# Shifting the start of each weight piece inside its buffers, in a gated-convolution layer on one core

## The chip, the cores and the metric

The kernel runs on one core of a Trainium2 chip. A core has a matrix engine (TensorE, in the profile PE for matmuls and PEld for the loading of the stationary operand), VectorE (DVE), ScalarE (ACT), GpSimd (POOL) and the queue processor SyncE (SP), which here issues all transfers (DMA) between the main memory and the on-chip memory. Matmuls write to eight accumulation banks. The metric is the device time of one execution in microseconds; the time before is the median of three runs.

## The reference

One layer of a decoder trunk, for 256 positions and a model width of 2048. In short, with `D = 2048`, `E = 4096`, one layer and float32 throughout:

```python
h = rmsnorm(x, norm_g)
mod = silu(c) @ ada_w + ada_b            # (1, 3*D): shift, scale, gate
h = h * (1 + scale) + shift
b_gate, c_gate, v, g = split(h @ w_in, 4)         # w_in (D, 4*E)
u = causal_depthwise_conv(c_gate * v, conv_w)     # three taps
y = (b_gate * u * silu(g)) @ w_out                # w_out (E, D)
out = rmsnorm(x + gate * y, final_g)
```

The large inputs are `w_in` (2048 x 16384), `w_out` (4096 x 2048) and `ada_w` (2048 x 6144), all float32. All the weights are read once.

## The kernel before

**Precision.** TensorE multiplies in a float32 form with a shortened mantissa (F32R). So each float32 operand is split into a high part, its rounded value, and a low part, the rest; the product is hi·hi + hi·lo + lo·hi, that is three matmuls' worth of columns. `split` does it for a piece of weights of up to 2048 floats per partition: ScalarE casts `raw` into `hi` (L191), VectorE subtracts `hi` from `raw` into `lo` (L192). `raw`, `hi` and `lo` have three buffers each. The normalized and modulated input lies transposed in `hT`, per block k of 128 channels first the 256 columns of the high part, then those of the low part.

**Stages.** At the start x is loaded, normalized (without shift and scale) and transposed by TensorE into `xs`. Then come three stages.

1. *mm_s*, the first 16 of 32 channel tiles of each quarter of `w_in`, in parts of four tiles (function `part`). A part runs over some range of k, so that it can begin before all of `hT` is known. Weights `hi` and `lo` are the stationary operand, `hT` streams in 256 columns: L286 (hi with the high half of hT), L291 (hi with the low half), L292 (lo with the high half). Partial sums are added up in `acc` (L298, L300). Meanwhile the adaLN product for shift and scale is computed on VectorE, from pieces `at` of `ada_w` (loaded at L231; multiplied by silu(c) and added into `gv` at L236 and L238), summed over partitions by transposing (L247) and accumulating on ScalarE (L249). A group of one or two blocks k is then scaled, shifted and split into `hT` (L258, L261, L262). The function `plan` writes the order of adaLN pieces and matmul parts out beforehand, by costs and due times of its own.
2. *mm_b*, the other 16 tiles, two tiles and one quarter at a time over all of k: L382 streams 512 columns of `hT` (both halves) against hi, L385 streams 256 against lo. The gating and convolution follow per pair of tiles. Between them stand the adaLN pieces for the gate (`at_g`, issued at L350, used at L357 and L359).
3. *mm_o*, the product with `w_out`. Here the roles change: `y` is the stationary operand and the weights stream in 512 columns: L427 (high part of y with hi), L428 (high part of y with lo), L429 (low part of y with hi). Then the gated residual and the last norm.

**Buffers.** On-chip memory is handed out pool after pool, from the left and from the right end. From the left: constants (`const`), then `adap` with two `gv` and four `at` buffers of 4 KB a partition, then `wpool` with three buffers each of `raw`, `lo` and `hi`, 8 KB a partition. From the right end down: `hpool` (32 KB: `hT`, later `big`) and `slots` (4 KB each: `xs`, `acc`, `y`, `z`, gates). In the first group of adaLN pieces (k0 = 0) the buffers of `lo` and `hi` serve as `at0`, since no weights need them yet. Nearly all of the memory is in use.

**Order.** Within each engine the order is fixed when the program is built, by a list scheduler that simulates the timeline; the scheduler also sees how many buffers a pool has. SP issues transfers in order, so that a transfer whose buffer isn't free yet holds up those behind it. The lines that matter here are L191 and L192 in `split`, L231 to L238 in `ada_piece`, L273 (load of `raw_s`), L350 (load of `at_g`), and the matmul lines above.

Of the kernel before, what the change touches and what calls it, by code (L numbers as in the profile page):

```python
# [8 lines left out]
F32 = mybir.dt.float32  # L9
F32R = mybir.dt.float32r  # L10
# [3 lines left out]
P = 128  # L14
# [20 lines left out]

SLOT = 2048
ASLOT = 1024
NSLOT = KT // CT + 4 * NCH


# [48 lines left out]
def short_conv_layer(ctx: ExitStack, tc: tile.TileContext, x, c, norm_g, ada_w, ada_b, w_in, conv_w, w_out, final_g, out):  # L89
    nc = tc.nc  # L90
    PSUM = bass.MemoryType.PSUM

    const = ctx.enter_context(tc.tile_pool(name="const", bufs=1))
    adap = ctx.enter_context(tc.tile_pool(name="adap", bufs=2))
    wpool = ctx.enter_context(tc.tile_pool(name="wpool", bufs=2))
    psum = ctx.enter_context(tc.tile_pool(name="psum", bufs=6, space=PSUM))
    hpool = ctx.enter_context(tc.tile_pool(name="hpool", bufs=1, side="right"))
    slots = ctx.enter_context(tc.tile_pool(name="slots", bufs=NSLOT, side="right"))

# [84 lines left out]
    shift = const.tile([P, KT], F32, tag="shift", name="shift")  # L184
    scale = const.tile([P, KT], F32, tag="scale", name="scale")

    def split(raw, n):

        hi = wpool.tile([P, SLOT], F32R, tag="hi", name="hi", bufs=3)
        lo = wpool.tile([P, SLOT], F32R, tag="lo", name="lo", bufs=3)  # L190
        nc.scalar.copy(hi[:, :n], raw[:, :n])  # L191
        nc.vector.tensor_tensor(out=lo[:, :n], in0=raw[:, :n], in1=hi[:, :n].bitcast(F32), op=ALU.subtract)  # L192
        return hi, lo
# [22 lines left out]
    def ada_piece(k0, nk, piece):  # L216
        w = nk * P
        kk = ASLOT // (2 * w)
        if piece == 0:
            sums[k0] = adap.tile([P, 2, 2 * P], F32, tag="gv", name="gv")  # L220
        gv = sums[k0]

        turns = [gv[:, :, i * w : (i + 1) * w] for i in range(2 if k0 == 0 and nk == 1 else 1)]
        j = piece * kk
        if k0 == 0:
            at = wpool.tile([P, SLOT], F32, tag=("lo", "hi")[piece % 2], name="at0", bufs=3)[:, :ASLOT]
        else:
            at = adap.tile([P, ASLOT], F32, tag="at", name="at", bufs=4)
        at4 = at.rearrange("p (k s f) -> p k s f", k=kk, s=2)
        for s in range(2):  # L230
            nc.sync.dma_start(at4[:, :, s, :], adas[:, j : j + kk, s, k0 * P : k0 * P + w])  # L231
        for i in range(kk):
            c_k = silu_c[:, j + i : j + i + 1]
            g2 = turns[(j + i) % len(turns)]
            if j + i < len(turns):
                nc.vector.tensor_scalar_mul(g2, at4[:, i], c_k)  # L236
            else:
                nc.vector.scalar_tensor_tensor(out=g2, in0=at4[:, i], scalar=c_k, in1=g2, op0=ALU.mult, op1=ALU.add)  # L238
        if j + kk < KT:
            return  # L240
        if len(turns) == 2:
            nc.vector.tensor_tensor(out=turns[0], in0=turns[0], in1=turns[1], op=ALU.add)

        tp = psum.tile([P, 4, P], F32, tag="sm", name="tp_g", bufs=2)
        gs = const.tile([P, 4], F32, tag="gs", name="gs", bufs=2)
        for o in range(2 * nk):
            nc.tensor.transpose(tp[:, o, :], gv[:, o // nk, (o % nk) * P : (o % nk + 1) * P], ident)  # L247
        for o in range(2 * nk):
            nc.scalar.activation(gjunk, tp[:, o, :], AF.Copy, accum_out=gs[:, o : o + 1])  # L249
        ks = slice(k0, k0 + nk)  # L250
        nc.vector.tensor_tensor(out=scale[:, ks], in0=gs[:, nk : 2 * nk], in1=b_scale[:, ks], op=ALU.add)
        nc.vector.tensor_tensor(out=shift[:, ks], in0=gs[:, 0:nk], in1=b_shift[:, ks], op=ALU.add)
        nc.vector.scalar_tensor_tensor(
            out=scale[:, ks], in0=scale[:, ks], scalar=1.0, in1=gT[:, ks], op0=ALU.add, op1=ALU.mult
        )
        for k in range(k0, k0 + nk):
            hf = xs[k // CT][:, k % CT, :]
            nc.vector.tensor_scalar(  # L258
                out=hf, in0=hf, scalar1=scale[:, k : k + 1], scalar2=shift[:, k : k + 1], op0=ALU.mult, op1=ALU.add
            )  # L260
            nc.scalar.copy(hh_[:, k], hf)  # L261
            nc.vector.tensor_tensor(out=hl_[:, k], in0=hf, in1=hh_[:, k].bitcast(F32), op=ALU.subtract)  # L262

    def part(ch, q, k0, k1):
# [4 lines left out]
        for s0 in range(k0, k1, step):  # L269
            sk = min(step, k1 - s0)  # L270
            n = sk * CT * P
            raw = raw_tile("raw_s")
            nc.sync.dma_start(  # L273
                raw[:, :n].rearrange("p (k f) -> p k f", k=sk),
                w_in[0, s0 * P : (s0 + sk) * P, col : col + CT * P].rearrange("(k p) f -> p k f", p=P),
            )
            hi, lo = split(raw, n)
            for i in range(sk):
                k = s0 + i
                hh, hl = hh_[:, k], hl_[:, k]  # L280
                for m in range(CT):
                    o = slice((i * CT + m) * P, (i * CT + m + 1) * P)
                    dst = banks[m // 2][:, (m % 2) * T : (m % 2 + 1) * T]

                    opens = k == k0 and m % 2 == 0
                    first = nc.tensor.matmul(dst, hi[:, o], hh, start=opens, stop=False, skip_group_check=True)  # L286
                    if opens:
                        opener = first
                    elif k == k0:
                        tc.add_manual_dep(first.ins, opener.ins.name, after, reason="the bank's flags are cleared first")  # L290
                    nc.tensor.matmul(dst, hi[:, o], hl, start=False, stop=False, skip_group_check=True)  # L291
                    nc.tensor.matmul(dst, lo[:, o], hh, start=False, stop=k == k1 - 1, skip_group_check=True)  # L292
# [25 lines left out]
    for kind, *step in plan():  # L318
        if kind == "ada":
            ada_piece(*step)  # L320
        else:
            ch, k1 = step[0], step[3]
            part(*step)
            whole[ch] += k1 == KT
            if k1 == KT and whole[ch] == 4:
                mixed(ch)
# [11 lines left out]
    def gate(dc):  # L338
        return gates[dc // 2][:, dc % 2, :]
# [4 lines left out]
    def gate_piece():  # L344
        if not gate_todo:
            return
        dc, j = gate_todo.pop(0)
        at = adap.tile([P, ASLOT], F32, tag="at", name="at_g", bufs=4)
        at3 = at.rearrange("p (k f) -> p k f", k=2)
        nc.sync.dma_start(at3, adas[:, j : j + 2, 2, dc * 512 : (dc + 1) * 512])  # L350
        if j == 0:
            gacc[0] = adap.tile([P, 512], F32, tag="gv", name="gacc")
        ga = gacc[0]
        for i in range(2):
            s = silu_c[:, j + i : j + i + 1]
            if j + i == 0:
                nc.vector.tensor_scalar_mul(ga, at3[:, i, :], s)  # L357
            else:
                nc.vector.scalar_tensor_tensor(out=ga, in0=at3[:, i, :], scalar=s, in1=ga, op0=ALU.mult, op1=ALU.add)  # L359
        if j + 2 == KT:  # L360
            ps = psum.tile([P, 512], F32, tag="sm", name="ps_gate", bufs=2)
            nc.tensor.matmul(ps, ones, ga, start=True, stop=True)  # L362
            nc.vector.tensor_tensor(out=gate(dc), in0=ps, in1=gate(dc), op=ALU.add)
# [3 lines left out]
    for ct in range(NS, NCT, 2):  # L367
        for q in QUARTERS:
            banks = [psum.tile([P, 2, T], F32, tag="mm", name="mm_b") for _ in range(2)]
            col = q * E + ct * P  # L370
            for kp in range(0, KT, KP):
                raw = raw_tile("raw")
                nc.sync.dma_start(
                    raw.rearrange("p (k f) -> p k f", k=KP),
                    w_in[0, kp * P : (kp + KP) * P, col : col + 2 * P].rearrange("(k p) f -> p k f", p=P),
                )
                hi, lo = split(raw, SLOT)
                for m in range(2):
                    for i in range(KP):
                        k = kp + i  # L380
                        o = slice((i * 2 + m) * P, (i * 2 + m + 1) * P)
                        nc.tensor.matmul(  # L382
                            banks[m].rearrange("p a t -> p (a t)"), hi[:, o], hT[:, k, :], start=k == 0, stop=False, skip_group_check=True
                        )
                        nc.tensor.matmul(banks[m][:, 0, :], lo[:, o], hh_[:, k], start=False, stop=k == KT - 1, skip_group_check=True)  # L385
                n_piece += 1
                if n_piece % 2 == 0:
                    gate_piece()
# [17 lines left out]
    while gate_todo:  # L406
        gate_piece()
# [41 lines left out]
    for dc in range(4):  # L449
# [8 lines left out]
        for ep in range(n_ep):  # L458
# [11 lines left out]
            hi, lo = split(raw, SLOT)  # L470
# [55 lines left out]
```

## Time and profile before

| | |
|---|---|
| median of three runs | 953.21 us (949.77 to 953.99) |
| profiled execution | 952.04 us, span 950.2 us, mean granted clock 0.99 |
| TensorE busy (matmuls) | 918.3 us, 97% of the span |
| weight loads busy | 835.4 us, 88% |
| VectorE, ScalarE busy | 681.4 us (72%), 419.3 us (44%) |
| transfers | 227.51 MB, mean 239 GB/s, 72.9% of the 16 DMA engines |
| mm_s, mm_b, mm_o | from 27 to 407 us, to 763 us, to 941 us |

How to read it: times are microseconds from the start of the span. A row of a group gives line, engine, operation, output and inputs by the program's names, shapes, count, then the busy time, the mean length of one in ns, and the idle time of the engine just before such instructions with what ended it. Matmuls are pipelined: the length of one reaches into the next, so the cost of a matmul in a row of them is the distance from its start to the next one's. The row of slices has one digit for each fortieth of the span, the busy share in tenths. In a row of windows stand the stretch, its length, busy time and count, the granted clock of TensorE, the share of the DMA engines in use and the rate.

### The profile page before, as it was taken

The numbers are of one execution on the slowest core, as the hardware profiler recorded it, in microseconds if no ns is written. First come the engines' busy times: TensorE is split into PE (matmuls) and PEld (weight loads), VectorE is DVE, ScalarE is ACT, GpSimd is POOL, SyncE is SP. The second block draws the span as 40 slices with busy tenths as digits, with TensorE's granted clock in tenths as the row PEclk, the third lists the DMA queues.
The fourth block names the chain that finished last, engine by engine and source line by source line (L and its number), as shares of the span: only waits on it lengthen the run. The fifth ranks groups of instructions, "written<-read, shape, count | busy, mean of one in ns | idle before, by whom it ended". The sixth has DMA issues, their size and how long they took to land.

```text
span 950.2 us, 14332 instructions
## 1 busy us (share of the span) xinstructions
PE 918.3 (97%) x5963; PEld 835.4 (88%) x5963; DVE 681.4 (72%) x789; ACT 419.3 (44%) x470; POOL 0.7 (0%) x6
## 2 busy tenths in 40 slices
PE   2799999999999999999999999999999999999996
PEld 2699999999999999988888888888888878888885
DVE  4799998999999998997465556555555654544882
ACT  6575343443435544444443444444444433343333
POOL 0000000000000000000000000000000000000000
PEclk9799999999999999999999999999999999999998
DMA  9999997999989787886665565566555685555542
GB/s 273 299 360 368 291 335 253 323 347 319 350 278 308 243 271 240 281 288 208 193 201 181 185 199 193 178 193 201 181 178 190 206 313 177 180 199 196 178 133 88
DMA packets 172048, 227.51 MB, mean 239 GB/s; under 512 B 5792, under 2 KB 112464, under 8 KB 171600
## 3 DMA queue, kind: packets, MB, share of 16 engines
q1 hardware_dynamic: 171984, 226.61, 72.9%
q8 instruction: 46, 0.75, 0.3%
q14 instruction: 18, 0.15, 0.0%
HBM read 224.49 MB, written 2.10 MB: 238 GB/s over the span
## 4 chain that ended last, share of the span: by engine, by line
PE 91%; DMA 4%; DVE 2%; issue 1%; SPq 1%; ACT 0%; ACTq 0%; DVEq 0%
PE mm_b L382 25%; PE mm_b L385 13%; PE mm_s L292 11%; PE mm_s L286 11%; PE mm_s L291 11%; PE mm_o L428 6%; PE mm_o L427 6%; PE mm_o L429 6%; DMA at<-in_ada_w_dram 2%; DMA raw_s<-in_sc_w_in_dram 2%; DVE lo L192 1%; DMA x<-in_x_dram 1%; DVE gv L238 1%; SPq L231 0%; PE ps_gate L362 0%
## 5 line engine op out<-in xcount | busy, mean ns | idle before, releaser
L382 PE MATMUL mm_b<-hT,hi 128*128 128x512 f32 x1024 | 355.2, 392 | 0.0
L286 PE MATMUL mm_s<-hT,hi 128*128 128x256 f32 x1024 | 286.9, 284 | 7.5 <-ACT hT L261 4.9
L291 PE MATMUL mm_s<-hT,hi 128*128 128x256 f32 x1024 | 287.7, 283 | 0.0
L385 PE MATMUL mm_b<-hT,lo 128*128 128x256 f32 x1024 | 285.4, 280 | 0.0
L292 PE MATMUL mm_s<-hT,lo 128*128 128x256 f32 x1024 | 283.6, 283 | 1.7 <-DVE lo L192 1.7
L192 DVE TENSOR_TENSOR lo<-raw,hi 128x2048 fp32r<-128x2048 f32 x64 | 146.6, 2291 | 128.4 <-ACT hi L191 128.4
L382 PEld LDWEIGHTS mm_b<-hT,hi 128*128 128x128 f32 x1024 | 192.0, 188 | 42.3 <-issue 0.2
L191 ACT CAST hi<-raw_s 128x2048 fp32r<-128x2048 f32 (+3 forms) x85 | 126.5, 1488 | 177.1 <-PE mm_s L291 128.6
L286 PEld LDWEIGHTS mm_s<-hT,hi 128*128 128x128 f32 x1024 | 194.4, 191 | 8.5 <-ACT hT L261 5.1
L291 PEld LDWEIGHTS mm_s<-hT,hi 128*128 128x128 f32 x1024 | 195.5, 191 | 0.2 <-issue 0.2
L292 PEld LDWEIGHTS mm_s<-hT,lo 128*128 128x128 f32 x1024 | 192.6, 191 | 2.6 <-DVE lo L192 2.4
L385 PEld LDWEIGHTS mm_b<-hT,lo 128*128 128x128 f32 x1024 | 192.3, 188 | 0.5 <-issue 0.2
L191 ACT CAST hi<-raw 128x2048 fp32r<-128x2048 f32 x64 | 122.4, 1912 | 158.0 <-PE mm_b L382 103.1
L192 DVE TENSOR_TENSOR lo<-raw_s,hi 128x2048 fp32r<-128x2048 f32 (+3 forms) x85 | 149.5, 1759 | 19.9 <-ACT hi L191 19.5
L192 DVE TENSOR_TENSOR lo<-raw_o,hi 128x2048 fp32r<-128x2048 f32 x32 | 73.3, 2290 | 67.0 <-ACT hi L191 67.0
L191 ACT CAST hi<-raw_o 128x2048 fp32r<-128x2048 f32 x32 | 61.2, 1913 | 103.8 <-PE mm_o L429 93.6
L428 PE MATMUL mm_o<-lo,y 128*128 128x512 f32 x256 | 101.7, 399 | 0.0
L427 PE MATMUL mm_o<-hi,y 128*128 128x512 f32 x256 | 101.0, 396 | 0.0
L429 PE MATMUL mm_o<-hi,y 128*128 128x512 f32 x256 | 100.1, 392 | 0.0
L238 DVE SCALAR_TENSOR_TENSOR gv<-at,silu_c,gv 128x512 f32<-128x512 f32 (+1 forms) x149 | 92.2, 639 | 3.8 <-DMA at<-in_ada_w_dram 3.0
L427 PEld LDWEIGHTS mm_o<-hi,y 128*128 128x128 f32 x256 | 48.1, 188 | 12.6 <-issue 0.2
L429 PEld LDWEIGHTS mm_o<-hi,y 128*128 128x128 f32 x256 | 48.1, 188 | 11.6
(84 smaller groups left out, 457.8 us busy)
## 6 DMA issues: line engine op xcount, KB each, us to landing
raw<-in_sc_w_in_dram SPq DMA_DIRECT2D x64, 1024.0 KB, 5.6
raw_s<-in_sc_w_in_dram SPq DMA_DIRECT2D x46, 1024.0 KB, 7.3
at<-in_ada_w_dram SPq DMA_DIRECT2D x128, 256.0 KB, 6.7
raw_o<-in_sc_w_out_dram SPq DMA_DIRECT2D x32, 1024.0 KB, 5.1
at_g<-in_ada_w_dram SPq DMA_DIRECT2D x32, 512.0 KB, 6.9
raw_s<-in_sc_w_in_dram SPq DMA_DIRECT2D x19, 512.0 KB, 5.4
raw_s<-in_sc_w_in_dram SPq DMA_DIRECT2D x7, 768.0 KB, 7.7
raw_s<-in_sc_w_in_dram SPq DMA_DIRECT2D x13, 256.0 KB, 4.4
```

Source lines behind the costliest of these rows:

```text
L191: nc.scalar.copy(hi[:, :n], raw[:, :n])
L192: nc.vector.tensor_tensor(out=lo[:, :n], in0=raw[:, :n], in1=hi[:, :n].bitcast(F32), op=ALU.subtract)
L238: nc.vector.scalar_tensor_tensor(out=g2, in0=at4[:, i], scalar=c_k, in1=g2, op0=ALU.mult, op1=ALU.add)
L286: first = nc.tensor.matmul(dst, hi[:, o], hh, start=opens, stop=False, skip_group_check=True)
L291: nc.tensor.matmul(dst, hi[:, o], hl, start=False, stop=False, skip_group_check=True)
L292: nc.tensor.matmul(dst, lo[:, o], hh, start=False, stop=k == k1 - 1, skip_group_check=True)
L382: nc.tensor.matmul(banks[m].rearrange("p a t -> p (a t)"), hi[:, o], hT[:, k, :], start=k == 0, stop=False, skip_group_check=True)
L385: nc.tensor.matmul(banks[m][:, 0, :], lo[:, o], hh_[:, k], start=False, stop=k == KT - 1, skip_group_check=True)
L427: nc.tensor.matmul(po, yh, hi[:, o], start=opens, stop=False, skip_group_check=True)
L428: nc.tensor.matmul(po, yh, lo[:, o], start=False, stop=False, skip_group_check=True)
L429: nc.tensor.matmul(po, yl, hi[:, o], start=False, stop=ct == NCT - 1, skip_group_check=True)
```

## The change

A piece of weights used to begin at the beginning of its `hi` and `lo` buffer. Now these buffers are 64 floats (256 bytes) longer, and a counter in `split` sets where a piece begins: `hi` at 0, 8, 16, ... 56 floats, a new place with each piece; `lo` at the same eight places, a new one with every eighth piece. There are 181 pieces in all, so all 64 pairs of places come up. The matmuls take their slices from the shifted view. To make room, the `at` buffers of adaLN are three where they were four. Two tiles that nothing uses are added: 224 bytes a partition at the right end of the memory, so that `hT` and the slots move down by that much, and 192 bytes after the constants, so that the pools from `adap` on move up.

```diff
+LEFT = 48
+LINE = 64
...
+    lines = ctx.enter_context(tc.tile_pool(name="lines", bufs=1, side="right"))
+    lines.tile([P, 56], F32, tag="end", name="end")
     const = ctx.enter_context(tc.tile_pool(name="const", bufs=1))
+    linel = ctx.enter_context(tc.tile_pool(name="linel", bufs=1))
+    linel.tile([P, LEFT], F32, tag="begin", name="begin")
     adap = ctx.enter_context(tc.tile_pool(name="adap", bufs=2))
...
+    n_split = [0]
+
     def split(raw, n):
 
-        hi = wpool.tile([P, SLOT], F32R, tag="hi", name="hi", bufs=3)
-        lo = wpool.tile([P, SLOT], F32R, tag="lo", name="lo", bufs=3)
+        o, n_split[0] = n_split[0], n_split[0] + 1
+        ho, lo = o % 8 * 8, o // 8 % 8 * 8
+        hi = wpool.tile([P, SLOT + LINE], F32R, tag="hi", name="hi", bufs=3)[:, ho : ho + SLOT]
+        lo = wpool.tile([P, SLOT + LINE], F32R, tag="lo", name="lo", bufs=3)[:, lo : lo + SLOT]
         nc.scalar.copy(hi[:, :n], raw[:, :n])
...
         if k0 == 0:
-            at = wpool.tile([P, SLOT], F32, tag=("lo", "hi")[piece % 2], name="at0", bufs=3)[:, :ASLOT]
+            at = wpool.tile([P, SLOT + LINE], F32, tag=("lo", "hi")[piece % 2], name="at0", bufs=3)[:, :ASLOT]
         else:
-            at = adap.tile([P, ASLOT], F32, tag="at", name="at", bufs=4)
+            at = adap.tile([P, ASLOT], F32, tag="at", name="at", bufs=3)
...
-        at = adap.tile([P, ASLOT], F32, tag="at", name="at_g", bufs=4)
+        at = adap.tile([P, ASLOT], F32, tag="at", name="at_g", bufs=3)
```

## The prediction

> **What bounds the kernel now.** First the page: busy shares, slices, the chain that ended last.
>
> ```profile
> span 950.2 us, 14332 instructions
> PE 918.3 (97%) x5963; PEld 835.4 (88%) x5963; DVE 681.4 (72%) x789; ACT 419.3 (44%) x470; POOL 0.7 (0%) x6
> ...
> PE   2799999999999999999999999999999999999996
> ...
> DVE  4799998999999998997465556555555654544882
> ...
> PE 91%; DMA 4%; DVE 2%; issue 1%; SPq 1%; ACT 0%; ACTq 0%; DVEq 0%
> ```
>
> TensorE is busy from the second slice to the last and holds 91% of the chain, so what is added to every matmul comes out at the end, and what is added elsewhere counts only once a matmul waits for it. VectorE is full for the first 16 slices or so: there, work that comes late may reach TensorE. Next the groups, shapes apart.
>
> ```profile
> L382 PE MATMUL mm_b<-hT,hi 128*128 128x512 f32 x1024 | 355.2, 392 | 0.0
> L291 PE MATMUL mm_s<-hT,hi 128*128 128x256 f32 x1024 | 287.7, 283 | 0.0
> L286 PE MATMUL mm_s<-hT,hi 128*128 128x256 f32 x1024 | 286.9, 284 | 7.5 <-ACT hT L261 4.9 <-ACT hi L191 2.6
> L385 PE MATMUL mm_b<-hT,lo 128*128 128x256 f32 x1024 | 285.4, 280 | 0.0
> L292 PE MATMUL mm_s<-hT,lo 128*128 128x256 f32 x1024 | 283.6, 283 | 1.7 <-DVE lo L192 1.7
> ...
> L428 PE MATMUL mm_o<-lo,y 128*128 128x512 f32 x256 | 101.7, 399 | 0.0
> L427 PE MATMUL mm_o<-hi,y 128*128 128x512 f32 x256 | 101.0, 396 | 0.0
> L429 PE MATMUL mm_o<-hi,y 128*128 128x512 f32 x256 | 100.1, 392 | 0.0
> ```
>
> The idle columns tell that matmuls hardly wait: 7.5 + 1.7 us for all that use hT. The means overlap one another, so the cost of one is the step from start to start. Stages by windows (columns: us, PE busy and count, granted clock, DMA share, GB/s):
>
> ```profile
> 28.60:33.00 4.40, 4.40 (x22) 0.50 0.81 243
> ...
> 420.00:670.00 250.00, 250.00 (x1444) 1.00 0.61 196
> 770.00:925.00 155.00, 155.00 (x666) 1.00 0.57 193
> ```
>
> A window also counts a matmul or two that reach over its edges. Then mm_b takes 250/1442 = 173.4 ns a matmul, 346.7 for a pair of 512 and 256 columns, and mm_o 155/664 = 233.4. For mm_s and for the pure streaming time I read starts in the timeline (start us, length; first and last of each run):
>
> ```profile
> 28.78 0.41 PE L291 MATMUL mm_s<-hT,hi 128*128 128x256 f32 x1
> ...
> 30.06 0.41 PE L292 MATMUL mm_s<-hT,lo 128*128 128x256 f32 x1
> ...
> 101.25 0.28 PE L292 MATMUL mm_s<-hT,lo 128*128 128x256 f32 x1
> ...
> 102.43 0.28 PE L286 MATMUL mm_s<-hT,hi 128*128 128x256 f32 x1
> ...
> 249.83 0.28 PE L292 MATMUL mm_s<-hT,lo 128*128 128x256 f32 x1
> ...
> 250.79 0.28 PE L291 MATMUL mm_s<-hT,hi 128*128 128x256 f32 x1
> ...
> 281.77 0.28 PE L292 MATMUL mm_s<-hT,lo 128*128 128x256 f32 x1
> ...
> 282.84 0.28 PE L292 MATMUL mm_s<-hT,lo 128*128 128x256 f32 x1
> ```
>
> Six steps at the granted clock 0.50 take 1.28 us, 213.3 ns each; at the full clock that is 106.7 ns for 256 columns and 213.3 for 512. At the full clock the three other runs show 1.18/10 = 118, 0.96/8 = 120 and 1.07/9 = 119 ns. So beside its streaming a matmul pays an extra: about 12.2 ns in mm_s, 26.7/2 = 13.3 in mm_b, 233.4 - 213.3 = 20 in mm_o. In all 3072 x 12.2 + 2048 x 13.3 + 768 x 20 = 37.5 + 27.2 + 15.4 = 80 us, which is all that any place of the operands could give back. The three rhythms of mm_s came with one layout, so places are not all that sets them.
>
> **The change part by part.** Sums stand against the profiled execution, 952.04 us with its span of 950.2; the median of the runs is 953.21, 1.2 higher.
>
> *What is not added.* No matmul, cast, subtraction or transfer is added or taken away; buffer counts of raw, hi and lo stay. The two unused tiles have no instruction. The cast (L191) and the subtraction (L192) write to shifted places with the same shapes; I cost that at nothing, for after the first 16 slices VectorE is busy four to six tenths, ScalarE is busy 44% of the span, and the waits for hi and lo above are all that ever reached a matmul.
>
> *Places.* Adding up the tiles by the code, hT and y begin today 32 bytes past a multiple of 64, hi and lo on one. Afterwards hT and y begin on a multiple of 256; a piece's hi and lo begin 0, 32, ... 224 bytes past one, so half the places lie on a multiple of 64 and half between. No row shows the same shape in another layout. The nearest: in mm_o the loaded side (y) lies between and the streamed side (hi, lo) on a multiple, at 20 ns; in mm_s and mm_b it is the other way round, at 12 to 13. Read that way, loading from between costs 20 - 12.2 = 7.8 ns in mm_s and 6.7 in mm_b: 3072 x 7.8 + 2048 x 6.7 = 38 us if all pieces paid it, 19 for the half that begin between. mm_o would gain 768 x 6.7 = 5, its loaded side now being on a multiple. That makes +14. The stages differ in width too, so the reading may be wrong and the price zero; I take half, **+7 us**. Ends: +38, all places as dear as mm_o; below, one step of 7 ns (L428's mean 399 less L429's 392) off each of the 5120 matmuls that stream hT, -36.
>
> *Three adaLN buffers.* Rows for the loop of one buffer:
>
> ```profile
> at<-in_ada_w_dram SPq DMA_DIRECT2D x128, 256.0 KB, 6.7
> ...
> L231 SPq DMA_DIRECT2D at<-in_ada_w_dram x128: 367/460/1427, 4.9 to 234.8; - x128
> ...
> 112.64 0.75 DVE L238 SCALAR_TENSOR_TENSOR gv<-at,silu_c,gv 128x512 f32<-128x512 f32 x1
> ...
> 113.42 0.88 SPq L231 DMA_DIRECT2D at<-in_ada_w_dram  x2
> ...
> 118.57 2.28 DVE L192 TENSOR_TENSOR lo<-raw_s,hi 128x2048 fp32r<-128x2048 f32 x1
> ...
> L238 DVE SCALAR_TENSOR_TENSOR gv<-at,silu_c,gv 128x512 f32<-128x512 f32 (+1 forms) x149 | 92.2, 639 | 3.8 <-DMA at<-in_ada_w_dram 3.0
> ...
> 55.00:250.00 195.00, 177.97 (x230) 1.00 0.97 325
> ```
>
> The issue at 113.42 starts as the vector operation of 112.64 ends (113.39): SP waits for the buffer. 64 pieces go out in 230 us, 3.6 us each, so a buffer's loop is 14.4 us with four buffers. Of it 0.9 is issue, 6.7 landing, two operations of 0.75 use: 9.1. The other 5.3 us the piece lies waiting for VectorE's turn. With three buffers the same pace leaves a loop of 10.8 and a wait of 1.7, which is less than one subtraction (2.28) ahead of it in VectorE's queue: short by 0.6 us a loop, 0.2 a piece, 10 us over the 50 pieces from 55 us on. Queued behind a late piece's operations are subtractions that feed TensorE, and behind its issue on SP are the raw_s loads; DMA is full there too (share 0.97), so a held-up issue isn't all made up for. Against it: VectorE still has 195 - 178 = 17 us idle in that stretch, and VectorE idled only 3.8 us for at with four. So 0 if VectorE's waiting takes all of it, 10 if nothing does; I take **+4 us**, close to what at costs VectorE today. The gate pieces use the same buffers, but their sums are read only in the output stage, which the last window above shows: nothing.
>
> Sum: 952.0 + 7 + 4 = **963 us**, 1.0% above the median of the runs.
>
> **The rivals.** *Places cost nothing.* For it: the three rhythms under one layout. Against it: mm_o's 20 ns. Time: 952 plus 0 to 4 for the buffers, 952 to 956, which I count as no change. The Trainium skill, page SBUF — State Buffer, section Door 1: The DMA port swizzle, says that consecutive accesses pay for each new 16-byte line; all places of the change are multiples of 32 bytes, so by that rule no stream touches more lines than before, and 956 would be the sum where mine is 963. Its page TensorE: Matmul & The Clock Gate, section Back-to-back issue gap, would give 109 ns for 256 columns; the trace has 118 to 120 and doesn't agree, so something that those rules leave out is at work.
>
> *Faster: hT on the boundary.* The matmuls that stream hT lose one 7 ns step wherever the loaded piece begins on a multiple of 64 too, in half the pieces: 2560 x 7 = 18 us, less the 4 of the buffers: 938. For it: today every one of these 5120 streams begins between two multiples, and the 7 ns step exists (L428 against L429). Against it: mm_o streams from a multiple and has the larger extra. It decides as soon as the step saved in some places outweighs what the others add, at an average of 1 ns a matmul (5 us).
>
> *Much slower: the places collide.* All eight are as dear as mm_o: 952 + 38 + 4 = 994; half of that price: 975. *adaLN becomes the bound* in the first 250 us: the 10 us in full and as much again because the raw_s loads behind it on SP land late: 952 + 7 + 20 = 979. For it the full VectorE slices; against it the idle 17 us.
>
> **How the numbers follow.** Forecast (slower by some, 957 to 975): 0.40. No change: 0.17. Faster: 0.27. Colliding places: 0.08; adaLN as the bound: 0.08. A measurement of this kernel tells about 0.5% from no change, 4.8 us. Slower is 0.40 + 0.08 + 0.08 = 0.56. For 8 in 10 the range runs from 938, the faster rival, to 982, beyond both the bound-by-adaLN case and half the colliding price; left out are the faster cases below 938 (some 0.12) and the full collision (some 0.06). The forecast's own range is 957 to 975.
>
> **What would show it.** Right: the same counts in every group; in the windows of mm_b more than 173.4 ns a matmul as a mean, with pieces that differ from one another by some 7 ns a matmul in step with their place (eight pieces for hi, eight times eight for lo); mm_o below 233.4. The buffers: L238 idle for at well above 3.8 us, SP waiting longer at L231, and idle before L286 or L292 above 9.2 us in all. Wrong: mm_b and mm_s unchanged to a ns (places cost nothing), or below 170 and 116 (hT's alignment was the extra). If matmuls wait for hT between 55 and 285 us by more than 10 us in all, the buffers weigh more than I allow.

## The result, and the profile after

The changed kernel takes 954.96 us as the median of 18 runs (952.94 to 958.48), against 951.96 us before in as many (949.77 to 953.99): a ratio of 1.0031, 95% interval 1.0020 to 1.0042. It is slower, by a third of what was forecast, outside the forecast's own range of 957 to 975, and by less than the 0.5% that the prediction had set as the limit of telling.

The page of the changed kernel: the span and the busy shares, then the chain by engine.

```profile
span 956.7 us, 14336 instructions
PE 921.8 (96%) x5963; PEld 836.2 (87%) x5963; DVE 683.0 (71%) x789; ACT 418.4 (44%) x470; POOL 0.7 (0%) x6
...
PE 85%; DVE 6%; DMA 5%; issue 2%; ACT 1%; SPq 0%; ACTq 0%; DVEq 0%
```

The profiled execution, at 958.48 us, happens to be the slowest of the 18, so its span exaggerates the change: 6.5 us where the medians differ by 3.0. TensorE's part of the chain fell from 91% to 85%, and VectorE and the transfers hold 11% where they held 6%: in places TensorE now waits for data. The groups show where (busy, mean ns, then idle before and its releaser):

```profile
L394 PE MATMUL mm_b<-hT,hi 128*128 128x512 f32 x1024 | 358.9, 395 | 0.0
L298 PE MATMUL mm_s<-hT,hi 128*128 128x256 f32 x1024 | 285.8, 284 | 7.7 <-ACT hi L203 4.0
L304 PE MATMUL mm_s<-hT,lo 128*128 128x256 f32 x1024 | 284.2, 284 | 6.0 <-DVE lo L204 6.0
...
L440 PE MATMUL mm_o<-lo,y 128*128 128x512 f32 x256 | 100.4, 393 | 0.0
...
L250 DVE SCALAR_TENSOR_TENSOR gv<-at,silu_c,gv 128x512 f32<-128x512 f32 (+1 forms) x149 | 93.9, 643 | 9.6 <-DMA at<-in_ada_w_dram 8.5
```

TensorE's idle time in mm_s is 7.7 + 6.0 = 13.7 us, before it was 9.2. VectorE waits 9.6 us for adaLN's pieces, before 3.8. Windows of TensorE alone (us, busy and count, granted clock, DMA share, GB/s):

```profile
100.00:150.00 50.00, 47.30 (x397) 1.00 0.91 294
...
345.00:400.00 55.00, 55.00 (x468) 1.00 0.79 258
420.00:670.00 250.00, 250.00 (x1431) 1.00 0.61 199
780.00:925.00 145.00, 145.00 (x627) 1.00 0.59 199
```

Between 100 and 150 us 2.7 us are idle, where before none were. In mm_b the step is 250/1429 = 174.9 ns (two of the count reach over the edges), before 173.4; in mm_o 145/625 = 232.0, before 233.4. From the starts of all matmuls in the timeline, without pauses: three of mm_s take 353.6 ns as a mean (before 355.9), a pair of mm_b 350.1 (346.7), three of mm_o 695.2 (700.0). That makes 1024 x -2.3 = -2.4 us, 1024 x 3.4 = +3.5 and 256 x -4.8 = -1.2: the places, summed over the stages, cost nothing. What is left in this execution is time lost in mm_s.

### The profile page after: what moved, and what is told of

Read it like the earlier page. It is cut to its first block, busy times and chain, and to the rows that moved or that the text cites. A ratio compares the mean times of both kernels' runs of the same rounds, so it can differ in the third digit from the quotient of the medians.

```text
span 956.7 us, 14336 instructions
## 1 busy us (share of the span) xinstructions
PE 921.8 (96%) x5963; PEld 836.2 (87%) x5963; DVE 683.0 (71%) x789; ACT 418.4 (44%) x470; POOL 0.7 (0%) x6
## 4 chain that ended last, share of the span: by engine, by line
PE 85%; DVE 6%; DMA 5%; issue 2%; ACT 1%; SPq 0%; ACTq 0%; DVEq 0%
PE mm_b L394 25%; PE mm_b L397 13%; PE mm_s L304 10%; PE mm_s L298 10%; PE mm_s L303 10%; PE mm_o L439 6%; PE mm_o L441 6%; PE mm_o L440 6%; DVE lo L204 2%; DMA raw_s<-in_sc_w_in_dram 2%; DMA at<-in_ada_w_dram 1%; DVE gv L250 1%; ACT hi L203 1%; DMA x<-in_x_dram 1%; DMA at_g<-in_ada_w_dram 1%
## 5 line engine op out<-in xcount | busy, mean ns | idle before, releaser
L394 PE MATMUL mm_b<-hT,hi 128*128 128x512 f32 x1024 | 358.9, 395 | 0.0
L440 PEld LDWEIGHTS mm_o<-lo,y 128*128 128x128 f32 x256 | 48.1, 188 | 11.4 <-issue 0.2
L439 PEld LDWEIGHTS mm_o<-hi,y 128*128 128x128 f32 x256 | 48.1, 188 | 11.4 <-issue 0.2
```

Of the source, the lines that this page charges most:

```text
L394: nc.tensor.matmul(banks[m].rearrange("p a t -> p (a t)"), hi[:, o], hT[:, k, :], start=k == 0, stop=False, skip_group_check=True)
L439: nc.tensor.matmul(po, yh, hi[:, o], start=opens, stop=False, skip_group_check=True)
L440: nc.tensor.matmul(po, yh, lo[:, o], start=False, stop=False, skip_group_check=True)
```

## The experiments

The theories at this point. *A:* the third adaLN buffer's loss costs all of it, and the places average out. *B:* the buffers are covered, the places cost it. Then, on what sets the step of a matmul: *P*, the pair of places of hi and lo; *Q*, the way in which a stage is entered; *R*, the distance between the place of the streamed operand and that of the loaded one; against R, the place of each against some multiple.

### Three buffers alone

```diff
-            at = adap.tile([P, ASLOT], F32, tag="at", name="at", bufs=4)
+            at = adap.tile([P, ASLOT], F32, tag="at", name="at", bufs=3)
```

and the same for `at_g`.

> The kernel before with one edit: three adaLN buffers in place of four, all places as before. Theory A (the places average out to about nothing, the buffers cost it all): 954.5 to 955, as the changed kernel, with TensorE idle some us more before L286 and L292 between 55 and 330 us, and mm_b still at 346.7 ns a pair. Theory B (the buffers are covered, the places cost the 3 us): 952 and no more idle time than the 9.2 us of before.

Measured: 957.02 us against 952.35, ratio 1.0051 (1.0034 to 1.0068), some 4.8 us. Two stretches of before and of this run (columns: us, then busy and count of PE, PEld, DVE, ACT, POOL, then the granted clock, DMA share, GB/s). Before:

```profile
25.00:55.00 30.00, 23.81 (x156) 22.91 (x157) 24.75 (x56) 18.62 (x37) 0.00 (x0) 0.80 1.00 310
...
100.00:150.00 50.00, 50.00 (x425) 50.00 (x424) 44.97 (x59) 20.00 (x22) 0.00 (x0) 1.00 0.89 286
```

Three buffers:

```profile
25.00:55.00 30.00, 23.92 (x138) 22.22 (x138) 23.29 (x49) 15.52 (x30) 0.00 (x0) 0.71 0.90 273
...
100.00:150.00 50.00, 47.25 (x396) 46.84 (x396) 45.52 (x64) 19.94 (x31) 0.00 (x0) 1.00 0.92 295
...
420.00:670.00 250.00, 250.00 (x1444) 220.16 (x1444) 152.61 (x152) 112.18 (x115) 0.00 (x0) 1.00 0.63 202
```

Here 29 matmuls fewer are done between 100 and 150 us, with 2.75 us idle. The changed kernel, which has three adaLN buffers too, shows the same there (397, 2.7 us idle), so this is the mark of the missing buffer. Before 55 us 18 matmuls fewer are done (about 2 us), but there the granted clock is at 0.71 in place of 0.80. The changed kernel, with three buffers and the clock at 0.81, had done 155 in the same window against 156 before, so that the early loss goes with the clock of this execution and can't be put down to the buffer. The changed kernel in that window:

```profile
25.00:55.00 30.00, 24.48 (x155) 22.84 (x156) 24.26 (x50) 17.06 (x32) 0.00 (x0) 0.81 0.93 292
```

mm_b counts 1444, exactly as before. That is theory A's half: the buffers alone cost at least what the whole change costs, 2 us more than A had expected.

### The places alone

Four adaLN buffers, all else as in the change. The room comes from small tiles that share memory; the core of it:

```diff
-            at = adap.tile([P, ASLOT], F32, tag="at", name="at", bufs=3)
+            at = adap.tile([P, ASLOT], F32, tag="at", name="at", bufs=4)
...
-    rows1 = const.tile([80, P], F32, tag="rows1", name="rows1")
-    rows2 = const.tile([96, P], F32, tag="rows2", name="rows2")
+    rows1 = const.tile([80, P], F32, tag="rows", name="rows1")
...
+    rows2 = const.tile([96, P], F32, tag="rows", name="rows2")
...
-    gjunk = const.tile([P, P], F32, tag="gjunk", name="gjunk")
+    gjunk = const.tile([P, P], F32, tag="rows", name="gjunk")
...
+    ones = const.tile([P, P], F32, tag="rows", name="ones")
```

> The change with its rotating places, but with four adaLN buffers; the room comes from small tiles that share memory (the two row tiles, the ones, the junk output of adaLN, two of the last norm's). Theory A (the buffers cost it all): the steps of the changed kernel (mm_s 353.5 ns for three, mm_b 350.1 a pair, mm_o 695.2 for three against 355.9, 346.7 and 700.0): -2.5, +3.5 and -1.2 us, and no more idle time between 60 and 410 us than before's 2.1: 951 to 953. Theory B (rotating places cost 2 to 3 us of their own): 954.5 or more.

Measured: 951.08 against 952.96, ratio 0.9984 (0.9974 to 0.9994). The steps are those of the changed kernel: 353.4, 350.1 and 695.2. Windows of TensorE and two groups:

```profile
100.00:150.00 50.00, 50.00 (x425) 1.00 0.87 281
...
420.00:670.00 250.00, 250.00 (x1429) 1.00 0.60 193
```

```profile
L300 PE MATMUL mm_s<-hT,lo 128*128 128x256 f32 x1024 | 284.8, 283 | 0.1
...
L246 DVE SCALAR_TENSOR_TENSOR gv<-at,silu_c,gv 128x512 f32<-128x512 f32 (+1 forms) x149 | 92.8, 642 | 1.8 <-DMA at<-in_ada_w_dram 1.1
```

TensorE waits 0.1 us for lo instead of 6.0, VectorE 1.8 us for adaLN's pieces instead of 9.6, and nothing is idle between 100 and 150 us. So theory A holds: +0.5% from the buffers, -0.16% from the places, and the sum is the +0.3% measured. Of the 1.5 us that the places gave, the steps hold only 0.1 (-2.4 + 3.5 - 1.2 above). The rest may be idle time or the small tiles that share memory in this run; that wasn't separated.

### One place for all pieces

In the changed kernel every one of the 64 pairs of places comes up as a piece of mm_b, and their steps differ: from 346.6 ns a pair of matmuls, at (0, 64) or (224, 96) bytes for instance, to 353.6. In mm_s the piece at (64, 192) was the quickest. Its starts in the timeline, the first and one near its end:

```profile
237.33 0.28 PE L298 MATMUL mm_s<-hT,hi 128*128 128x256 f32 x1
...
242.55 0.28 PE L303 MATMUL mm_s<-hT,hi 128*128 128x256 f32 x1
```

46 steps in 5.22 us, 113.5 ns each, where no rhythm of before was under 117. The pieces at (64, 64), at 97 and 397 us, ran at that pace too, the first of them for most of its length. Two kernels hold every piece at one place:

```diff
-        ho, lo = o % 8 * 8, o // 8 % 8 * 8
+        ho, lo = 0, 0
```

> The changed kernel with every piece at place 0 of both buffers (three adaLN buffers, everything on multiples of 256 bytes). Theory P (the step from matmul to matmul is fixed by the two places): as the pieces at (0, 0) in the changed kernel, mm_b 353 ns a pair and mm_s 120 a matmul, so 1024 x 6.5 + 3072 x 1.2 ns = 10 us above before and 2.6 more for the buffers: about 965. Theory Q (the rhythm is set by how a stage or a piece is entered, not by places): mm_b and mm_s as means near 350 and 118.5, about 955.

and with `ho, lo = 16, 16`, that is 64 bytes:

> The changed kernel with every piece 64 bytes into both buffers. Theory P: mm_s 113.5 ns a matmul (before 118.9), mm_b 352.6 a pair (before 346.7): -3072 x 5 + 1024 x 6 ns = -9 us, and 2.6 for the buffers: about 945. Theory Q: about 955, mm_s between 117.4 and 120.

Measured: 953.42 us (1.0012, 0.9999 to 1.0026) and 952.52 us (1.0004, 0.9989 to 1.0018), both with three adaLN buffers. Windows of TensorE at (0, 0):

```profile
345.00:400.00 55.00, 55.00 (x461) 1.00 0.77 242
420.00:670.00 250.00, 250.00 (x1445) 1.00 0.63 201
780.00:925.00 145.00, 145.00 (x641) 1.00 0.56 190
```

and at (64, 64):

```profile
345.00:400.00 55.00, 55.00 (x488) 1.00 0.84 273
420.00:670.00 250.00, 250.00 (x1417) 1.00 0.60 195
780.00:925.00 145.00, 145.00 (x635) 1.00 0.57 191
```

The two kernels differ in the places of hi and lo alone, and every stage moves: 461 against 488 matmuls in the same 55 us of mm_s, 1445 against 1417 in mm_b (346.8 and 353.3 a pair), 641 against 635 in mm_o (680.0 and 686.7 for three, where before took 700.0). P was right on mm_s at (0, 0), 360.0 for three throughout, and on mm_b at (64, 64). It was wrong on mm_b at (0, 0): 353 was expected from the one piece there, 346.8 came, so that a piece among others at other places doesn't have the step of its place alone. And it was half right on mm_s at (64, 64), which changes between 117.8 and 113.3 ns a matmul: the quicker rhythm holds for 54% of the steps, and the mean is 346.0 for three. Neither of P's times came, 965 at (0, 0) and 945 at (64, 64). At (64, 64) the changes of rhythm fall together with pauses of TensorE or with matmuls of adaLN in between. So a pair of places allows more than one rhythm, and how the stage is entered seems to pick: Q has a part in it, but no run set the entry on purpose.

### Distance, or place

```diff
+    linel = ctx.enter_context(tc.tile_pool(name="linel", bufs=1))
+    linel.tile([P, 56], F32, tag="begin", name="begin")
     adap = ctx.enter_context(tc.tile_pool(name="adap", bufs=2))
```

on the kernel with three buffers alone. hi and lo then begin 32 bytes past a multiple of 256, hT and y stay 224 past one.

> The kernel before with three adaLN buffers, and one unused tile of 224 bytes after the constants, so that hi and lo begin 32 bytes past a multiple of 256 while hT and y stay where they were, 224 past one. The distance from hT to the weights is then 64 bytes as with everything 64 bytes in, but no operand begins on a multiple of 64 ... of hT's own. Theory R (what counts is the distance between the streamed and the loaded operand): the steps of the run at (64, 64): mm_s 341 to 346 ns for three, mm_b 353.3 a pair, mm_o 686.7 for three; in all about 952.5. Theory B (what counts is where each begins against a multiple of 64 or 256): other steps than those, near the ones of before if hT's start decides (355, 346.7), and about 957.

Measured: 956.54 us (1.0037, 1.0021 to 1.0054).

```profile
345.00:400.00 55.00, 55.00 (x488) 1.00 0.83 270
420.00:670.00 250.00, 250.00 (x1417) 1.00 0.61 196
780.00:925.00 145.00, 145.00 (x635) 1.00 0.59 201
```

The three counts are those of the run at (64, 64), to the last one: 488, 1417, 635 (353.3 a pair in mm_b, 686.7 for three in mm_o). The window of mm_s shows the quicker rhythm; both runs have the slower one too, 117.8 ns, for 8% of the steps here and 44% there, so that their means differ, 341.2 and 346.0 for three. There all operands began on a multiple of 64, here none does; the distance from hT to the weights is 64 bytes in both. And no operand's place sets the step alone: at (0, 0) and (64, 64) hT has the same place and the steps differ; before and at (64, 64) the weights have the same place, 64 bytes past a multiple of 256, and the steps differ. Theory R holds, and a start on or between multiples of 64 has no part in the step, as far as this one distance in mm_s and mm_b and one in mm_o, each at two places, can show it.

The time, 4 us above the run at (64, 64), isn't in these windows. TensorE's idle time in mm_s is 9.3 + 8.9 us against 7.4 + 6.5 there, and in this execution two pauses, of 2.1 and 1.2 us, are followed by 3.4 us each in which the granted clock is half. The first of them, here and in the run at (64, 64):

```profile
119.90:123.30 3.40, 3.40 (x18) 0.51 0.94 276
```

```profile
119.90:123.30 3.40, 3.25 (x29) 1.00 0.98 345
```

The matmuls take 213 ns there in place of 113, some 1.7 us lost each time. A pause of 1.8 us at (64, 64), at 124 us, was not followed by a lower clock; what decides is open.

### One pair of places for each stage

```diff
-            hi, lo = split(raw, n)
+            hi, lo = split(raw, n, (16, 16))
...
-                hi, lo = split(raw, SLOT)
+                hi, lo = split(raw, SLOT, (0, 16))
...
-            hi, lo = split(raw, SLOT)
+            hi, lo = split(raw, SLOT, (48, 32))
```

> The changed kernel with one pair of places for each stage, those that were cheap in the changed kernel: (64, 64) bytes for mm_s, (0, 64) for mm_b, (192, 128) for mm_o. Theory P: mm_s 113.5 ns a matmul, mm_b 346.6 a pair, mm_o 688 for three (before 700): -16.5, 0 and -3 us, and 2.6 for the buffers: about 936. Theory Q: about 955.

> As the kernel with one pair of places for each stage, but mm_o at (0, 0). The run with everything at (0, 0) took 680.0 ns for three matmuls of mm_o, the one at (192, 128) 686.9. Theory P (places fix the step): mm_o 680, 256 x 6.9 ns = 1.8 us less than 946.2, so about 944. Theory Q (the rhythm is set by how a stage is entered): mm_o near 687, no change.

Measured: 946.20 us (0.9943, 0.9920 to 0.9965) and 945.38 us (0.9922, 0.9905 to 0.9938). mm_b kept 346.7 and mm_o went to 686.9 and 680.1 as P had it, but the first expectation was missed by 10 us. Three of mm_s took 343.6 ns where 340.5 was expected, 3 us in all, since both rhythms of (64, 64) occur again. And with three buffers the quicker matmuls of mm_s wait for their operands. In the group rows their idle time is 8.2 + 8.1 us in the first of the two, 7 more than before (the profiled execution, at 950.17 us, is the slowest of its four):

```profile
L298 PE MATMUL mm_s<-hT,hi 128*128 128x256 f32 x1024 | 284.4, 283 | 8.2 <-ACT hT L273 4.2 <-ACT hi L203 3.7 <-DVE acc L312 0.3
L304 PE MATMUL mm_s<-hT,lo 128*128 128x256 f32 x1024 | 282.8, 282 | 8.1 <-DVE lo L204 7.9
```

So the same places were put on the kernel with four buffers:

> Four adaLN buffers as in the run before this one, and one pair of places for each stage: (64, 64) in mm_s, (0, 64) in mm_b, (0, 0) in mm_o. If the adaLN buffers are what holds TensorE up in mm_s once its step is shorter: 5 us below the same places with three buffers, or more, since idle time of 16 us between 60 and 410 us is to be had there: 935 to 940. If VectorE and the transfers bind mm_s whatever the buffers: 942 to 944, with idle time that stays above 10 us.

Measured: 941.49 us (0.9863, 0.9841 to 0.9886), 1.5 us short of what was expected. That is 3.9 us less than the same places with three buffers. The waits for lo are gone, but now the slower of the two rhythms at (64, 64) held most of mm_s, and the mean is 350.0. Windows of TensorE:

```profile
250.00:300.00 50.00, 50.00 (x427) 1.00 0.93 314
345.00:400.00 55.00, 55.00 (x488) 1.00 0.86 282
```

50/425 = 117.6 ns in the first stretch, 55/486 = 113.2 in the second, with the same places (117.8 and 113.3 from start to start). The change came at 319 us, where a matmul of the gate stands between. Two more pairs for mm_s, `(16, 48)` and `(48, 32)` floats:

> As the run with four buffers and a pair of places for each stage, but mm_s at (64, 192), whose one piece in the changed kernel ran at 113.4 ns a matmul. If that pair has the quick rhythm alone: 340 ns for three through mm_s instead of 350 as a mean, 1024 x 10 ns = 10 us less than 941.5, unless VectorE and the transfers then hold TensorE up (idle time of over 5 us between 60 and 410 us, and 936 to 941). If every pair has two rhythms and the entry decides: anything from 340 to 354, 932 to 945.

> As the run with four buffers and a pair of places for each stage, but mm_s at (192, 128), whose pieces in the changed kernel ran at 115.8 to 116.9 ns a matmul. If places fix the step: 347 to 350 ns for three, the same time as (64, 64) reached there, 940 to 942. If the distance from hT to the low part (128 here, 64 there) doesn't count and the entry does: 340 or 354 as there.

Measured: 932.61 us, ratio 0.9792 (0.9767 to 0.9817), and 938.91 us, 0.9863 (0.9848 to 0.9879). At (64, 192):

```profile
250.00:300.00 50.00, 50.00 (x444) 1.00 0.93 316
```

```profile
L294 PE MATMUL mm_s<-hT,hi 128*128 128x256 f32 x1024 | 283.2, 280 | 6.7 <-ACT hT L269 3.8 <-ACT hi L199 2.9
L300 PE MATMUL mm_s<-hT,lo 128*128 128x256 f32 x1024 | 280.2, 278 | 1.7 <-DVE lo L200 1.7
```

340.2 ns for three all through mm_s, and no more than 8.4 us idle. This is the fastest version, 2.1% below before. Its steps explain the gain: 1024 x 15.7 ns in mm_s and 256 x 20 in mm_o would give 21 us, and 19 were measured. At (192, 128) three take 348.0 ns, within the 347 to 351 that its pieces had in the changed kernel. At (64, 192) one rhythm held nearly throughout, as at (0, 0). At (64, 64) two occur, and at (192, 128) more than one: there the trace has 115.5 ns a matmul for most of mm_s and 117.8 for some stretches.

## Why the prediction was wrong

The forecast was 963 us, 1.0% above; measured is +0.3%. The direction was right because of the buffers alone; the size was three times too large because of the places.

- *What bounds the kernel:* right. All counts stayed, and the place shows only in TensorE's steps and in its waits.
- *Three adaLN buffers, +4 us (0 to 10):* right. Alone they cost 4.8 us, and the places by stage lost 3.9 by the third buffer (945.4 against 941.5). The signs that were named came in the changed kernel: VectorE idle for adaLN's pieces 9.6 us instead of 3.8, TensorE idle 13.7 instead of 9.2, and 2.7 us of it between 100 and 150 us, in the stretch that the estimate was made for. The 4 was a choice between 0 and 10 and not a sum, so its closeness is partly luck. SP's wait for a free buffer grew only a little (rows of before, then after; total, times, longest):

```profile
SPq L231 <- DVE gv L238: 34.8, 36, 2.7
```

```profile
SPq L243 <- DVE gv L250: 40.8, 43, 2.7
```

- *Places, +7 us:* this is the step that failed. It came out at -1.5 us. The reading that loading from between two multiples costs 20 - 12.2 ns took mm_o's larger extra as the price of where y begins against a multiple of 64. The run shifted by 32 bytes refutes that: with all operands between the multiples or all on them, at the same distance, the steps are the same. mm_o's 20 ns came with the distance of 160 bytes from its streamed to its loaded operand; at distance 0 it is 13.3 (680.0/3 - 213.3). So the mm_o part of the term (-5) had the right sign, -1.2, since most distances are cheaper than the one it had. mm_b happened to stand near its best before, 346.7 against 346.6 for the best of 64 pairs, and lost 3.5 us by the mean over all; mm_s stood above the mean and gained 2.4. The mean over many distances is no price of any one of them, and the prediction had no row at a second distance in the same stage.
- *The rivals:* the one where places cost nothing (0.17) named the right time, 952 to 956, for a wrong reason, and that is luck: they matter by up to 6% in a stage, and cancel in a rotation. By the rule of the Trainium skill that was cited there (page SBUF — State Buffer, section Door 1: The DMA port swizzle), an access pays when it crosses to a new 16-byte line, and that makes all places of the change alike. The runs show that something else counts here: every place was a multiple of 32 bytes, and mm_s went from 340 to 360 ns for three. The faster rival (hT on the boundary) had the wrong mechanism, but its remark that one step of 7 ns can be saved held: 340.2/3 = 113.4 is 106.7 + 6.7, and 360.0/3 = 120.0 is 106.7 + 13.3.
- *What would show it:* mm_b above 173.4 and mm_o below 233.4 came. The pieces of mm_b differ by up to 7 ns a pair, where some 7 ns a matmul was named, and not in step with their place alone: the one piece at (0, 0) took 353 a pair, and with all pieces at (0, 0) they took 346.8.

What stays open: why the distance counts at all, why one pair of distances has one rhythm and another two, and which entry leads to which.

## What to carry to other kernels

Where a matmul streams and loads 4-byte operands without a break, it is worth shifting the buffers against each other and reading the step from start to start: here 2% lay in 64 to 192 bytes of padding, a different pair for each stage, and the rotation over all places served to find them, not to keep. Price a buffer that is given up for room by the wait it used to hide: one of four cost 0.5% here, more than the places gave on average. A price taken from another stage is no price; look for the same stage at a second value of what changes, or keep the term at zero with wide ends.

## What the runs showed of the hardware

- The step of back-to-back matmuls depends on the distance between the start of the streamed and of the loaded operand in their partitions, modulo 256 bytes as far as tried: 113.4 to 120.0 ns for 256 columns in mm_s with one place held, 346.7 to 353.3 for a pair in mm_b, 226.7 to 233.4 for 512 columns in mm_o. The same distance at another place gave the same counts (488, 1417 and 635); one distance was tried so in mm_s and mm_b, and one in mm_o.
- In the steadiest rhythms the extra is 6.7 ns (at (64, 192)) or 13.3 (at (0, 0)) over the streaming time of 106.7 for 256 columns, and 13.3 over 213.3 for 512. 6.7 ns is the time of 16 columns by that streaming time. Other rhythms lie between, 115.5, 117.8 and 118.6 ns for instance, so the steps of 6.7 are no rule.
- One layout can have two stable rhythms (113.3 and 117.8 ns at (64, 64)). With four buffers the slower one held from 50 to 318 us and the quicker one from there to the end of mm_s, some 80 us. Matmuls of adaLN stood within the first stretch without changing it. The changes seen at (64, 64) came with pauses of TensorE or with another kind of matmul in between, but not each of these brought one.
- A stage that gets quicker matmuls needs its operands sooner: with three adaLN buffers the same places by stage gave 945.4 us and 15.2 us of idle time in mm_s, 7.9 of it for lo; with four, 941.5 us and none of the wait for lo.
- A pause of TensorE can be followed by 3.4 us at a granted clock of 0.50, with 213 ns in place of 113 for a matmul of 256 columns (run shifted by 32 bytes, at 119.9 and 181.4 us). A pause of 1.8 us at (64, 64) was not.
